# Attention in plain float32: unsplit operands for scores and values, the values' heads on halves of the columns

## The chip, the core and the metric

The kernel runs on one core of one Trainium2 chip. The core has a matrix engine, TensorE (PE in the profile, PEld for its weight loads), a vector engine (DVE), a scalar engine that also applies functions (ACT), GpSimd (POOL) and SyncE (SP), which here issues the transfers. The metric is the device time of one execution in microseconds (us). Before the change it is 951.21 us, the median of three runs from 950.32 to 952.36.

## What is computed

Two decoder layers over 256 tokens of width 1024, one sequence. Each layer is a half-step SwiGLU FFN, a token mixer, and another half-step FFN; the mixer of the first layer is stick-breaking attention, that of the second a gated linear recurrence. The part that is changed is the attention, with 16 heads of 64:

```python
q = qkv[0] * (SB_HEAD_DIM ** -0.5)
k, v = qkv[1], qkv[2]
for blk in range(S // Q_BLOCK):
    z = einsum('bhqd,bhkd->bhqk', q[:, :, t0:L], k[:, :, :L])
    log_keep = where(mask, log_sigmoid(-z), 0.0)
    later = cumsum(log_keep, axis=3, reverse=True) - log_keep
    w = where(mask, exp(log_sigmoid(z) + later), 0.0)
    outs.append(einsum('bhqk,bhkd->bhqd', w, v[:, :, :L]))
...
return o @ w_o
```

`Q_BLOCK` is 128, so there are two blocks. The product of queries and keys is called scores here, the product of the weights `w` and the values `v` is called values.

## The kernel before

Everything is float32. A projection multiplies a weight by an activation, and each is kept as a rounded part and a rest (`wh`, `wl` and the like, both in the type fp32r that PE streams in one pass). A product is then three matmuls, high by high, high by low and low by high, all into the same PSUM bank. The rounded part is written by ACT, the rest by DVE. Helpers do this: `load` for weights (L582 on ACT, L585 on DVE), `split` for activations, `Acc.group` for the three matmuls (L611). A product can also be given to PE in plain float32, with no split; the gates of the second layer do so (L1301).

Tokens lie along the columns: a tile is 128 channels by 256 tokens (T). Heads go in pairs, since two heads of 64 channels fill 128 partitions; tile `f` holds pair `f` (0 to 7), and `c` counts pairs of pairs (0 to 3), four heads. Keys and values come in two blocks of 128. The first block of keys serves all 256 queries, the second only the last 128, so each product comes in a wide form (256 columns) and a short one (128).

In `attention`:

- `q_proj(f)` projects queries and keys of pair `f`, and writes them as a high and a low tile (ACT, then DVE at L1069 or L1082).
- `v_proj(fp)` projects the values of four heads (L1042), and `v_out` writes them high and low (DVE at L1055).
- `scores(c)` first puts a mask into four PSUM banks (L1114), then adds the products of queries and keys (L1130): for each pair and block three matmuls for each of the two heads. A head has 64 channels, so the one head's operands sit on partitions 0 to 63 and the other's on 64 to 127; the two alternate and write to different banks. Then comes `softplus` (ACT and DVE).
- `sums(c, e)` adds the running sums into the same banks as a product with a triangle of ones (L1160, L1163), takes the exponential on ACT, and splits the resulting weights (ACT, and DVE at L1176).
- `values(f)` multiplies the values of both heads of pair `f`, 128 columns of stationary operand, by the weights of both heads side by side (L1190): three matmuls for each of the two blocks, 512 and 256 columns. Only the half in which head and weights belong together is used. ACT and DVE (L1198) copy that half out, high and low, once for each head.
- `down` is the output projection. It begins when some of the heads are done; `tail` puts the last values in behind its second weight tile.

What sets the order: the code records operations with a cost in nanoseconds each, and `Program.schedule` then places them engine by engine, by due times that follow from PE's recorded order and by when inputs and buffers come free. The costs are the third thing in each `pr.op` call. `hook(f)` records loads of modulation weights (`rawm`), each of which SP issues in its place and DVE reads (L645). SP's queue carries all weights (`raw`, three buffers, and `rawm`, four) in one order.

Of the kernel before, what the change touches and what calls it, by code (L numbers as in the profile page):

```python
# [14 lines left out]
P = 128  # L15
T = 256
# [27 lines left out]
SKIP = 1  # L44

# [361 lines left out]
def trunk(ctx, tc, first_in, cb, par, modw, gu, wdn, qk, wv, wo, win, wri, wout, out):  # L407
# [12 lines left out]
    def f32(ap):  # L420
        return ap.bitcast(F32)
# [589 lines left out]
    def attention(l, s, nxt, hook):  # L1011
        R, F = new_phase(94, 24)
# [36 lines left out]
        def v_out(fp):  # L1049
            acc, _ = vs[fp]  # L1050
            b = acc.b
            y = Buf(R, 4, name=f"vh{fp}"), Buf(R, 4, name=f"vl{fp}")
            rd = [(b, 0), (b, 1)]
            A(y[0], b, AF.Copy, 512, rd, [y[0]], psum=True)
            V(lambda: dve.tensor_tensor(y[1](), b(), f32(y[0]()), ALU.subtract), 512, rd + [y[0]], [y[1]])  # L1055
            vs[fp] = y
# [4 lines left out]
        def q_proj(f):  # L1061
            if f == 0:
                firsts.append(up_first((l, s), [q_load(i) for i in range(NFIRST)], (0.125, 1.0)))
            y = qs[f] = Buf(R, 4, name=f"qh{f}"), Buf(R, 4, name=f"ql{f}")
            if f < NFIRST:
                def put(g, t, rd, c):
                    cols = slice(g * T, (g + 1) * T)
                    A(lambda: y[0]()[:, cols], t, AF.Identity, T, [t, rd], [(y[0], g)], ptr=1, bias=c)
                    V(lambda: dve.scalar_tensor_tensor(y[1]()[:, cols], t(), c(), f32(y[0]()[:, cols]), ALU.add,  # L1069
                                                       ALU.subtract), T, [t, rd, (y[0], g)], [(y[1], g)])  # L1070

                for g, v in enumerate(next(firsts[0])):
                    put(g, *v)
                return
            acc = Acc(f"qk{f}")
            up(acc, q_load(f), (l, s), True)

            def put2(g, scale):
                b, rd = acc.b, (acc.b, (g, 0))
                cols = slice(g * T, (g + 1) * T)  # L1080
                A(lambda: y[0]()[:, cols], lambda: b()[:, cols], AF.Copy, T, [rd], [(y[0], g)], psum=True, scale=scale)
                V(lambda: dve.scalar_tensor_tensor(y[1]()[:, cols], b()[:, cols], scale, f32(y[0]()[:, cols]), ALU.mult,  # L1082
                                                   ALU.subtract), T, [rd, (y[0], g)], [(y[1], g)])

            for g in range(2):
                put2(g, (0.125, 1.0)[g])
# [14 lines left out]
        def scores(c):  # L1101
# [20 lines left out]
            def products():  # L1122

                for j, (qh, ql) in enumerate(pairs):
                    for i, (kc, qc) in enumerate(((slice(T, T + P), slice(0, T)), (slice(T + P, 2 * T), slice(P, T)))):
                        m = NC[i] // 2
                        for n, (v, w) in enumerate(((qh, qh), (qh, ql), (ql, qh))):
                            for e in range(2):
                                rows = slice(e * 64, (e + 1) * 64)
                                pe.matmul(zb[e][i]()[:, j * m : (j + 1) * m], v()[rows, kc], w()[rows, qc], start=False,  # L1130
                                          stop=j == 1 and n == 2, skip_group_check=True)

            pr.op("PE", 460.0 + 510.0 * len(fs), products, [q for r in pairs for q in r], [z for zz in zb for z in zz])
# [17 lines left out]
        def sums(c, e):  # L1151
            sp_ = ws_.pop((c, e))
            w = Buf(F, 6, name=f"w{c}{e}")
# [17 lines left out]
            if e == 0:  # L1171
                os_[c, "w"] = Buf(R, 12, name=f"wh{c}"), Buf(R, 12, name=f"wl{c}")
            y = os_[c, "w"]
            cols = slice(e * W2, (e + 1) * W2)
            A(lambda: y[0]()[:, cols], w, AF.Copy, W2, [w], [(y[0], e)])
            V(lambda: dve.tensor_tensor(y[1]()[:, cols], w(), f32(y[0]()[:, cols]), ALU.subtract), W2, [w, (y[0], e)], [(y[1], e)])  # L1176
# [406 lines left out]
```

## Time and profile before

| | |
|---|---|
| median of three runs | 951.21 us |
| the profiled execution's own time | 950.51 us |
| its span, first to last instruction | 948.7 us |
| PE busy | 938.9 us (99%) |
| DVE busy | 794.2 us (84%) |
| ACT busy | 568.2 us (60%) |
| granted PE clock, mean | 0.997 |
| attention (about 197 to 312 us), L1130, L1190, L1160 on the chain | 1%, 1%, 1% of the span rounded |

The chain of waits is followed back from the last instruction: at each step to what released it, or to the instruction ahead of it on its engine. A row of the chain gives the start and the length of a piece in us, then the engine, the tile, the line and how many instructions it holds. Rows of the timeline give the same with tiles and shapes; a matmul's own length there includes its way through the array, so the distance between starts tells what one costs. In rows by line, three numbers with strokes are the shortest, median and longest duration in ns. The waits of SP's queue name what held a transfer back: total us, times, longest.

### The profile page before, as it was taken

Reading aid. Unit: us, or ns where it says so; the run is one execution under the profiler, and the core shown is the slowest. Engines: PE = TensorE matmul, PEld = TensorE weight load, DVE = VectorE, ACT = ScalarE, POOL = GpSimd, SP = SyncE. Lnnn points to the kernel's source line nnn. Section 1 sums busy time; section 2 is a strip of 40 time slices with the busy share of each in tenths; the row PEclk is TensorE's granted clock in tenths of the full one; section 3 lists DMA queues with packets and bytes.
Section 4 is the critical chain, followed back from the end, with each engine's and each line's share of the span. In section 5 each row is a group of like instructions: output and inputs, shape, how many; then the busy total and the mean of one; then the engine's idle time right before and its main releaser. Section 6 shows DMA issues by size and latency. Waiting matters only on the chain.

```text
span 948.7 us, 19727 instructions
## 1 busy us (share of the span) xinstructions
PE 938.9 (99%) x8110; PEld 929.4 (98%) x8110; DVE 794.2 (84%) x1304; ACT 568.2 (60%) x934; POOL 2.4 (0%) x15
## 2 busy tenths in 40 slices
PE   8999999999999999999999999999999999999997
PEld 7999999999999999999999999999999999999996
DVE  8999987899999999888889998865999997555443
ACT  6784544488887755454367555535789676544343
POOL 1000000000000000000000000000000000000000
PEclk9999999999999999999999999999999999999998
DMA  9989989857744699989967998886253646545431
GB/s 366 404 327 371 349 330 358 326 206 278 266 145 168 227 341 346 344 320 347 351 236 285 354 361 326 333 335 233 89 181 131 223 175 242 206 180 204 170 113 45
DMA packets 48332, 251.25 MB, mean 265 GB/s; under 512 B 5361, under 2 KB 5745, under 8 KB 28530
## 3 DMA queue, kind: packets, MB, share of 16 engines
q1 hardware_dynamic: 47952, 249.59, 70.2%
q8 instruction: 63, 1.03, 0.4%
q10 hardware_dynamic: 290, 0.40, 0.1%
q14 instruction: 27, 0.22, 0.1%
HBM read 248.92 MB, written 1.05 MB: 263 GB/s over the span
## 4 chain that ended last, share of the span: by engine, by line
PE 97%; DVE 2%; DMA 1%; issue 0%; ACT 0%; SPq 0%; DVEq 0%
PE bank L611 90%; PE bank L1042 2%; PE bank L1301 1%; PE bank L1190 1%; PE bank L917 1%; PE bank L1130 1%; DVE wl L585 1%; PE bank L1160 1%; DMA arenar<-in_first_in 1%; DVE arenar L645 0%; DVE x L1413 0%; PE bank L1163 0%; PE bank L1114 0%; DVE arenaf L1385 0%; PE bank L704 0%
## 5 line engine op out<-in xcount | busy, mean ns | idle before, releaser
L611 PE MATMUL bank<-hx,wh 128*128 128x256 f32 (+1 forms) x3264 | 560.5, 277 | 0.2 <-DVE hx L941 0.2
L582 ACT ACTIVATE wh<-raw 128x1024 fp32r<-128x1024 f32 (+1 forms) x330 | 335.4, 1037 | 282.0 <-PE bank L611 191.9
L611 PEld LDWEIGHTS bank<-hx,wh 128*128 128x128 f32 x3264 | 493.7, 188 | 0.5 <-DVE hx L941 0.4
L585 DVE TENSOR_TENSOR wl<-raw,wh 128x1024 fp32r<-128x1024 f32 (+1 forms) x330 | 387.4, 1197 | 103.0 <-ACT wh L582 99.4
L611 PE MATMUL bank<-hx,wl 128*128 128x256 f32 (+1 forms) x1640 | 452.7, 277 | 0.0
L611 PEld LDWEIGHTS bank<-hx,wl 128*128 128x128 f32 x1640 | 308.3, 188 | 0.0
L611 PE MATMUL bank<-arenar,wh 128*128 128x256 f32 x1696 | 289.4, 276 | 0.0
L611 PEld LDWEIGHTS bank<-arenar,wh 128*128 128x128 f32 x1696 | 255.6, 188 | 0.0
L611 PE MATMUL bank<-arenar,wl 128*128 128x256 f32 x848 | 234.3, 276 | 0.1
L645 DVE SCALAR_TENSOR_TENSOR rawm<-rawm,cact 128x1024 f32<-128x1024 f32 x128 | 155.4, 1221 | 20.2 <-DMA rawm<-in_modw 20.1
L611 PEld LDWEIGHTS bank<-arenar,wl 128*128 128x128 f32 x848 | 159.3, 188 | 0.3 <-DVE wl L585 0.3
L554 ACT ACTIVATE arenar<-a 128x256 fp32r<-128x256 f32 x88 | 35.3, 405 | 11.8 <-DVE a L870 10.3
L875 DVE TENSOR_TENSOR arenar<-a,arenar 128x256 fp32r<-128x256 f32 x88 | 36.4, 421 | 0.5 <-ACT arenar L554 0.5
L554 ACT ACTIVATE sg<-bank 128x256 f32<-128x256 f32 x82 | 29.8, 367 | 9.6 <-PE bank L611 9.5
L870 DVE TENSOR_TENSOR a<-bank,sg 128x256 f32<-128x256 f32 x82 | 34.2, 420 | 0.4 <-ACT sg L554 0.2
L785 DVE SCALAR_TENSOR_TENSOR x<-bank,mf,x 128x256 f32<-128x256 f32 (+1 forms) x49 | 21.8, 475 | 9.2 <-PE bank L611 9.1
L554 ACT ACTIVATE hx<-x,mf 128x256 fp32r<-128x256 f32 x40 | 19.3, 499 | 16.3 <-DVE x L785 16.3
L554 ACT ACTIVATE hx<-hpre,mf 128x256 fp32r<-128x256 f32 x41 | 19.9, 502 | 11.0 <-DVE hpre L731 9.6
L1042 PE MATMUL bank<-wh,hx 128*128 128x256 f32 x128 | 23.4, 281 | 0.0
L645 DVE SCALAR_TENSOR_TENSOR arenar<-arenar,cact 128x1024 f32<-128x1024 f32 x16 | 19.5, 1222 | 1.6 <-DMA arenar<-in_first_in 1.6
L554 ACT ACTIVATE arenaf<-bank 128x512 f32<-128x512 f32 (+1 forms) x37 | 17.0, 512 | 6.0 <-DVE arenaf L1372 1.8
L1523 ACT ACT_TABLE_LOAD x15 | 19.2, 1283 | 1.6 <-PEq L1571 1.4
(130 smaller groups left out, 550.4 us busy)
## 6 DMA issues: line engine op xcount, KB each, us to landing
raw<-in_gu SPq DMA_DIRECT2D x79, 1024.0 KB, 5.2
rawm<-in_modw SPq DMA_DIRECT2D x128, 512.0 KB, 7.0
raw<-in_wdn SPq DMA_DIRECT2D x44, 1024.0 KB, 5.2
raw<-in_win SPq DMA_DIRECT2D x10, 1024.0 KB, 4.9
arenar<-in_first_in SPq DMA_DIRECT2D x16, 512.0 KB, 8.3
raw<-in_qk SPq DMA_DIRECT2D x8, 1024.0 KB, 4.8
raw<-in_wout SPq DMA_DIRECT2D x5, 1024.0 KB, 4.9
raw<-in_first_in SPq DMA_DIRECT2D x8, 512.0 KB, 8.9
```

The costliest lines, as they stand in the source:

```text
L554: act.activation(o(), i(), f, **{k: (v() if callable(v) else v) for k, v in kw.items()})
L582: act.activation(h()[:, :m], raw()[:, a : a + m], AF.Copy)
L585: dve.tensor_tensor(lo()[:, :m], raw()[:, a : a + m], f32(h()[:, :m]), ALU.subtract)
L611: pe.matmul(o(b()), wc(u()), xc(v()), start=start and n == 0, stop=stop and n == len(passes) - 1, skip_group_check=True)
L645: dve.scalar_tensor_tensor(raw(), raw(), 1.0, cact(), ALU.mult, ALU.mult, accum_out=m()[:, t : t + 1])
L785: dve.scalar_tensor_tensor(x[d]()[:, w], acc.b()[:, j * T + w.start : j * T + w.stop], gate()[:, d : d + 1], x[d]()[:, w], ALU.mult, ALU.add)
L870: V(lambda: dve.tensor_tensor(a(), b()[:, T:], sg(), ALU.mult), T, [(b, (1, 0)), sg], [a])
L875: V(lambda: dve.tensor_tensor(y[1](), a(), f32(y[0]()), ALU.subtract), n, [a, y[0]], [y[1]])
L917: pr.op("PE", c_mm(T, 4), lambda: pe.matmul(b()[:, g * T : (g + 1) * T], raw()[:, c0 : c0 + P], h0(), start=start, stop=False, skip_group_ ...
L1042: pe.matmul(o, u()[:, tb * P : (tb + 1) * P], v()[:, c0 : c0 + 256], start=start and n == 0, stop=k == KD - 1 and n == 2, skip_group_check ...
L1130: pe.matmul(zb[e][i]()[:, j * m : (j + 1) * m], v()[rows, kc], w()[rows, qc], start=False, stop=j == 1 and n == 2, skip_group_check=True)
L1523: act.preload_act_table_set(TABLES[t])
```

## The change

Scores are computed by one plain float32 matmul for each head, pair and block in place of three split ones; queries and keys are no longer split, so ACT alone writes them. The values and the attention weights are not split either. `values` is called once for four heads and writes one PSUM bank: for each pair and block, each head's 64 values are the stationary operand, on columns 0 to 63 or 64 to 127 of the array, multiplied by that head's weights only; the two heads alternate. The outputs are evicted and split in one piece of 128x512. The two buffers of the phase change size, the costs given to the planner are two constants, and the calls stand in another order.

```diff
+SCORES = 1400.0
+VALUES = 1350.0
...
-        R, F = new_phase(94, 24)
+        R, F = new_phase(50, 68)
...
         def v_out(fp):
-            y = Buf(R, 4, name=f"vh{fp}"), Buf(R, 4, name=f"vl{fp}")
-            rd = [(b, 0), (b, 1)]
-            A(y[0], b, AF.Copy, 512, rd, [y[0]], psum=True)
-            V(lambda: dve.tensor_tensor(y[1](), b(), f32(y[0]()), ALU.subtract), 512, rd + [y[0]], [y[1]])
-            vs[fp] = y
+            y = vs[fp] = Buf(F, 4, name=f"v{fp}")
+            A(y, b, AF.Copy, 512, [(b, 0), (b, 1)], [y], psum=True)
...
             def products():
 
-                for j, (qh, ql) in enumerate(pairs):
+                for j, y in enumerate(pairs):
                     for i, (kc, qc) in enumerate(((slice(T, T + P), slice(0, T)), (slice(T + P, 2 * T), slice(P, T)))):
                         m = NC[i] // 2
-                        for n, (v, w) in enumerate(((qh, qh), (qh, ql), (ql, qh))):
-                            for e in range(2):
-                                rows = slice(e * 64, (e + 1) * 64)
-                                pe.matmul(zb[e][i]()[:, j * m : (j + 1) * m], v()[rows, kc], w()[rows, qc], start=False,
-                                          stop=j == 1 and n == 2, skip_group_check=True)
-
-            pr.op("PE", 460.0 + 510.0 * len(fs), products, [q for r in pairs for q in r], [z for zz in zb for z in zz])
+                        for e in range(2):
+                            rows = slice(e * 64, (e + 1) * 64)
+                            pe.matmul(zb[e][i]()[:, j * m : (j + 1) * m], y()[rows, kc], y()[rows, qc], start=False, stop=j == 1,
+                                      skip_group_check=True)
+
+            pr.op("PE", SCORES, products, pairs, [z for zz in zb for z in zz])
...
-            A(lambda: y[0]()[:, cols], w, AF.Copy, W2, [w], [(y[0], e)])
-            V(lambda: dve.tensor_tensor(y[1]()[:, cols], w(), f32(y[0]()[:, cols]), ALU.subtract), W2, [w, (y[0], e)], [(y[1], e)])
-
-        def values(f):
-            wh, wl = os_[f // 2, "w"]
-            vh, vl = vs[f // 2]
+
+        def values(c):
+
+            ww = [ws_.pop((c, e, "w")) for e in range(2)]
+            v = vs[c]
             b = Buf(banks)
 
             def fn():
-                for tb in range(2):
-                    vc = slice(tb * T + (f % 2) * P, tb * T + (f % 2 + 1) * P)
-                    o = b() if tb == 0 else second(b())
-                    m = NC[tb] // 2
-                    at = BL[tb].start + (f % 2) * m
-                    for i, (u, v) in enumerate(((vh, wh), (vh, wl), (vl, wh))):
-                        pe.matmul(o, u()[:, vc], v().rearrange("p (e s) -> p e s", e=2)[:, :, at : at + m],
-                                  start=tb == 0 and i == 0, stop=i == 2, skip_group_check=True)
-            pr.op("PE", c_mm(512) + c_mm(T), fn, [vh, vl] + [(q, e) for q in (wh, wl) for e in range(2)], [b])
...
+                for j in range(2):
+                    for tb in range(2):
+                        at = BL[tb].start + j * NC[tb] // 2
+                        for e in range(2):
+                            vc = tb * T + j * P + e * 64
+                            pe.matmul(b()[e * 64 : (e + 1) * 64, j * T + tb * P : (j + 1) * T], v()[:, vc : vc + 64],
+                                      ww[e]()[:, at : at + NC[tb] // 2], start=j == tb == 0, stop=j == tb == 1,
+                                      skip_group_check=True)
+            pr.op("PE", VALUES, fn, [v] + [(w, i) for w in ww for i in range(2)], [b])
+            y = Buf(R, 4, name=f"oh{c}"), Buf(R, 4, name=f"ol{c}")
+            A(y[0], b, AF.Copy, 512, [b], [y[0]], psum=True)
+            V(lambda: dve.tensor_tensor(y[1](), b(), f32(y[0]()), ALU.subtract), 512, [b, y[0]], [y[1]])
+            for j in range(2):
+                os_[2 * c + j] = y, slice(j * T, (j + 1) * T)
...
         sums(2, 1)
         q(7)
         scores(3)
+        values(2)
         v_proj(3)
```

What this does to the order of the instructions is seen at three places. The first is on PE, where the scores of the last two pairs are computed, `scores(3)`. Before, part of the last value projection (L1042, `wh` and `wl` with `hx`) stands between the masks (L1114) and the products (L1130); banks 70, 68, 67 and 69 take the scores.

```order
L1114 MATMUL bank_69<-mask,ident 128x256
L1042 MATMUL bank_64<-wh_81,hx 128x256
...
L1042 MATMUL bank_64<-wh_81,hx 128x256
L1130 MATMUL bank_70<-arenar_2524 128x256
L1130 MATMUL bank_68<-arenar_2524 128x256
L1130 MATMUL bank_70<-arenar_2524 128x256
L1130 MATMUL bank_68<-arenar_2524 128x256
L1130 MATMUL bank_70<-arenar_2524 128x256
L1130 MATMUL bank_68<-arenar_2524 128x256
L1130 MATMUL bank_67<-arenar_2524 128x128
```

After, at the same place, with L1104 the masks, L1173 the values of pairs 4 and 5 and L1119 the scores of pairs 6 and 7:

```order
L1104 MATMUL bank_65<-mask,ident 128x256
L1173 MATMUL bank_70<-arenaf_2525 64x256 x2
L1173 MATMUL bank_70<-arenaf_2525 64x128 x2
L1173 MATMUL bank_70<-arenaf_2525 64x256 x2
L1173 MATMUL bank_70<-arenaf_2525 64x128 x2
L1119 MATMUL bank_63<-arenaf_2525 128x256
L1119 MATMUL bank_69<-arenaf_2525 128x256
L1119 MATMUL bank_67<-arenaf_2525 128x128
L1119 MATMUL bank_65<-arenaf_2525 128x128
L1119 MATMUL bank_63<-arenaf_2525 128x256
L1119 MATMUL bank_69<-arenaf_2525 128x256
L1044 MATMUL bank_66<-wh_81,hx 128x256
```

The values moved to directly ahead of the scores' products, and the value projection (L1044, L1042 before) begins behind them.

The second place is on PE in the output projection, around the last values. Before, with L1190 the values of pair 7 and L611 the projection's steps (`wh_80` to `wh_83` with their `wl` are the last four of its eight weight halves; the first step that needs pair 7 has `wh_83`):

```order
L1190 MATMUL bank_66<-arenar_2524 128x512 x3
L1190 MATMUL bank_66<-arenar_2524 128x2x128 x3
L611 MATMUL bank_65<-arenar_2524,wh_80 128x256 x2
...
L611 MATMUL bank_65<-arenar_2524,wh_82 128x256 x2
...
L611 MATMUL bank_65<-arenar_2524,wh_83 128x256 x2
```

After, with L1173 the values of pairs 6 and 7 and L613 the steps (the first that needs pair 6 has `wh_82`):

```order
L1173 MATMUL bank_69<-arenaf_2525 64x256 x2
L1173 MATMUL bank_69<-arenaf_2525 64x128 x2
L613 MATMUL bank_67<-arenar_2524,wh_78 128x256 x2
...
L613 MATMUL bank_67<-arenar_2524,wh_79 128x256 x2
...
L613 MATMUL bank_64<-arenar_2524,wh_80 128x256 x2
...
L613 MATMUL bank_64<-arenar_2524,wh_81 128x256 x2
...
L613 MATMUL bank_64<-arenar_2524,wh_80 128x256 x2
...
L613 MATMUL bank_64<-arenar_2524,wh_82 128x256 x2
```

Between the last values and the first step that needs them stand seven steps of three matmuls before, and five after.

The third place is on SP's queue, at the loads of the last value projection (`wv`) and of the output projection (`wo`). Before (L547) and after (L549):

```order
L547 DMA raw_73<-in_wv 128x2048
L547 DMA rawm_76<-in_modw 128x1024
L547 DMA rawm_77<-in_modw 128x1024
L547 DMA raw_71<-in_wo 128x2048
L547 DMA raw_72<-in_wo 128x2048
```

```order
L549 DMA raw_73<-in_wv 128x2048
L549 DMA rawm_74<-in_modw 128x1024
L549 DMA rawm_75<-in_modw 128x1024
L549 DMA rawm_76<-in_modw 128x1024
L549 DMA raw_71<-in_wo 128x2048
L549 DMA rawm_77<-in_modw 128x1024
L549 DMA raw_72<-in_wo 128x2048
```

Two more modulation tiles (`rawm`) stand ahead of the second `wo` load than before. Further up and down the queue single `rawm` loads have changed places with `raw` loads in the same way; no load is added or removed.

More of the change, by code (lines that the diff above doesn't have):

```diff
@@ L1228, in attention @@
         q(6)
-        values(2)
+        values(1)
         sums(2, 0)
-        values(3)
         sums(2, 1)
```

45 lines of the change are left out of this document (11 added, 34 removed).

## The prediction

> **What bounds the kernel now.** I read the page first, for the engine that carries the span, then the stretch in which attention runs, then the chain of waits inside it. Engines, the clock row and the chain by engine:
>
> ```profile
> PE 938.9 (99%) x8110; PEld 929.4 (98%) x8110; DVE 794.2 (84%) x1304; ACT 568.2 (60%) x934; POOL 2.4 (0%) x15
> ...
> PE 97%; DVE 2%; DMA 1%; issue 0%; ACT 0%; SPq 0%; DVEq 0%
> ```
>
> TensorE (PE) carries 97% of the chain. Attention lies between 197 and 312 us; busy time in that stretch:
>
> ```profile
> core 0: us, PE busy (x) PEld busy (x) DVE busy (x) ACT busy (x) POOL busy (x), PEclk, DMA share, GB/s
> 197.40:312.40 115.00, 115.00 (x993) 111.80 (x992) 109.29 (x192) 96.04 (x173) 0.00 (x0) 1.00 0.57 204
> ```
>
> PE is busy for all 115.00 us at full clock. DVE, at 109.29 of them, comes near, but PE never waits for it. So here time is gained or lost only by what PE's own instructions take, unless a new wait appears. The chain shows the groups that the change touches (start, length, line, count), and, from the second layer, plain float32 products (L1301):
>
> ```profile
> 210.08 5.49 PE bank L611 x48
> 215.57 0.45 PE bank L1114 x4
> 216.03 1.52 PE bank L1130 x24
> 217.55 5.69 PE bank L611 x48
> ...
> 249.45 1.05 PE bank L1190 x6
> ...
> 690.61 1.73 PE bank L1301 x8
> 692.34 5.49 PE bank L611 x48
> ```
>
> A projection's matmul of 256 columns (L611) takes 5.49/48 = 0.114 us. The 24 matmuls of the scores (L1130), half of them 256 wide and half 128, would take 12 x 0.114 + 12 x 0.057 = 2.06 us one after the other; they took 1.52, and the 48 behind them 0.20 longer than usual. Rows of the timeline in short windows around that group show both things (start, length):
>
> ```profile
> 215.65 0.38 PE L1114 MATMUL bank<-mask,ident 128*128 128x256 bf16 x2
> ...
> 215.75 0.27 PE L1114 MATMUL bank<-mask,ident 128*128 128x256 bf16 x1
> 215.96 0.38 PE L1130 MATMUL bank<-arenar 64*128 64x256 f32 x2
> ...
> 216.18 0.40 PE L1130 MATMUL bank<-arenar 64*128 64x256 f32 x4
> ...
> 216.41 0.33 PE L1130 MATMUL bank<-arenar 64*128 64x128 f32 x4
> ...
> 216.47 0.39 PE L1130 MATMUL bank<-arenar 64*128 64x128 f32 x4
> ...
> 216.58 0.44 PE L1130 MATMUL bank<-arenar 64*128 64x128 f32 x4
> ...
> 217.27 0.27 PE L1130 MATMUL bank<-arenar 64*128 64x128 f32 x2
> ...
> 217.48 0.38 PE L611 MATMUL bank<-hk,wh 128*128 128x256 f32 x1
> ...
> 217.70 0.28 PE L611 MATMUL bank<-hk,wh 128*128 128x256 f32 x1
> ```
>
> First, "x2" at 215.96: the two heads of a pair, on the upper and the lower 64 rows, run abreast. Second, going in and out of halves costs. In: last mask to first pair 0.21 instead of the 0.10 between masks, first to second pair 0.22 instead of 0.114. Out: 0.21 from the last pair, after 0.11 between short pairs, then 0.22 instead of 0.114. That is about 0.20 at either boundary. From the last mask (215.75) to the second L611 (217.70) are 1.95 us; less one mask (0.11) and one L611 (0.12) a scores group costs **1.72**, of it 0.39 boundaries and 1.33 stream.
>
> **The change part by part.** Scores: for each group of four heads 24 split matmuls become 8 plain ones. A plain product of 256 columns is two records; L1301's eight records take 1.73, so 0.216 each and 0.43 a product. No row has a plain product of 128 columns. It costs between half (0.22) and as much as the wide one (0.43). I take half, since the short pairs above stand 0.06 to 0.11 apart where wide ones stand 0.114: width does shorten the stream. If both heads run abreast as in L1130, a group streams 2 x (0.43 + 0.22) = 1.30, with boundaries 1.69: 0.03 less than 1.72, times 4 is **-0.1**. The ends: 0.29 more each if the two heads run staggered (below, +1.2); with the short product at 0.43, 0.43 more each (+1.7).
>
> Values: before, a call (L1190) is 1.05 for two heads, so 2.10 us for a group of four, on the full array without a boundary; it computes each head's values against both heads' weights and throws half away. After, eight plain products for a group, each on 64 of the columns. Abreast they stream 1.30, like the scores. Row halves run abreast in the rows above, column halves are in no row, so the ends are 1.30 abreast and 2 x 2 x (0.43 + 0.22) = 2.60 in turn. I take abreast: the nearest row is L1130, the array halved the other way. The boundary too is in no row: between 0 and the 0.39 of L1130; I take 0.39. So 1.69 against 2.10, times 4 is **-1.6** (ends: -3.2 without boundaries, +3.6 in turn with them). As the order shows, the values of the third group stand right ahead of the scores of the fourth, which joins two boundaries into one: **-0.2** (end 0).
>
> The Trainium skill (TensorEngine Tiling (Array Packing), Key Properties) says that changing the tiling mode drains the engine. The rows in and out of L1130 agree, at 0.2 us a boundary. By that rule the column halves pay as the row halves do and the sum is the one here; were it to hold for rows alone, the sum would be 1.6 lower.
>
> Splits that go: the weights' (L1176), the values' (L1055), the keys' and queries' (L1082, L1069); outputs' (L1198) become four of 128x512; rows by line:
>
> ```profile
> L1176 DVE TENSOR_TENSOR arenar<-arenaf,arenar x8: 947/958/959, 233.3 to 287.9; 128x768 fp32r<-128x768 f32 x8
> ...
> L1055 DVE TENSOR_TENSOR arenar<-bank,arenar x4: 685/689/693, 217.2 to 284.1; 128x512 fp32r<-128x512 f32 x4
> ...
> L1198 DVE TENSOR_TENSOR arenar<-bank,arenar x16: 408/420/429, 253.1 to 297.1; 64x256 fp32r<-64x256 f32 x16
> ...
> L1082 DVE SCALAR_TENSOR_TENSOR arenar<-bank,arenar x12: 405/422/425, 218.9 to 272.0; 128x256 fp32r<-128x256 f32 x12
> ```
>
> On DVE that frees 8 x 0.958 + 4 x 0.689 + 12 x 0.422 + 16 x 0.420 = 22.2 us (and four queries' splits more), less 4 x 0.689 = 2.8 for the new ones. ACT loses eight copies of 128x768 and twelve small evictions. All of it counts **0**: PE waited for neither engine in these 115 us, and it does not come back as time. It buys slack instead: transfers in this stretch mostly wait for DVE to release a weight buffer, so they can start earlier.
>
> ```profile
> SPq L547 <- DVE wl L585: 95.8, 19, 11.3
> SPq L547 <- DVE rawm L645: 19.1, 12, 3.4
> ```
>
> Moved transfers: on SP's queue some modulation tiles now go ahead of the last query/key, output-projection and next-FFN weights; each must find its buffer read by DVE (L645, longest wait 3.4). Cost 0 while the three weight buffers run ahead; bounded by one such wait on PE, +3.4, and not below 0, since PE waits for no transfer here.
>
> Down projection: the last values group must reach the seventh head pair's step. Before, the last one left PE at 295.75 and its last split ended at 297.06 + 0.43:
>
> ```profile
> 294.69 1.05 PE bank L1190 x6
> 295.75 1.26 PE bank L611 x11
> ...
> 297.06 0.43 DVE L1198 TENSOR_TENSOR arenar<-bank,arenar 64x256 fp32r<-64x256 f32 x1 [0.38 <-ACT arenar L554]
> ```
>
> That is 1.74 us of latency for four small evictions. Now one eviction and one split (0.69) of 512 stand there, and PE has five steps of three matmuls (15 x 0.114 = 1.71) plus the 0.2 of the boundary as cover. Cost 0, at worst one weight split (about 1.2) in the way.
>
> **Sum**: -0.1 - 1.6 - 0.2 = -1.9 us. The profiled execution took 950.51 (span 948.7); the median of the runs is 951.21, 0.70 above it, so I forecast 951.21 - 1.9 = **949.3**, which is 0.2% less, on the edge of what a measurement of this kernel tells from no change (about 1.9 us; its three runs spread over 2.0).
>
> **The rivals.**
> *Staggered halves.* A plain product is two records, and the first head's two stand ahead of the second head's. If matmuls start strictly in order, the second head cannot start before the first head's second record, and with widths that alternate they never close up: counting in records of 0.108, starts fall so that eight products end after 15 instead of 12, i.e. 1.62. Then scores cost 2.01 (+0.29), values 2.01 (-0.09): 4 x 0.20 - 0.2 = +0.6, so 951.8, no change. For it: two records for one product are in L1301's count. Against it: nothing, but L1130's pairs are single records and cannot show it. The Trainium skill (TensorE: Matmul & The Clock Gate, Part 3) says that matmuls keep program order in start and end; by that rule this is the outcome, and no row here decides whether it holds across halves.
> *No boundary for column halves.* L1190's neighbours in the new order are projections, as L1130's were, so I would expect one; without it 951.21 - 0.1 - 3.2 = 947.9, faster.
> *Columns in turn*, on the other side. If the second head's products cannot stream while the first's do, values cost 2.60 + 0.39 = 2.99 per group against 2.10, +3.6 in all, and -0.3 for the rest makes 954.5; with staggered scores 955.7. It turns to slower once a values group takes more than about 2.6. For it: two streams then enter over the same 128 rows, where L1130's used 64 each. Against: the outputs are separate.
> *A new wait* at the down projection or the moved transfers: +1.2 to +3.4, so 950.5 to 952.7. Against: DVE has some 20 us less to do there.
>
> **How the numbers follow.** Forecast (abreast, boundaries paid) 0.34, taken half on each side of the edge but for a little more on the faster one; no boundary 0.20; staggered 0.23; columns in turn 0.18; a new wait 0.05. Faster: 0.20 + 0.22 = 0.42. Same: 0.12 + 0.22 = 0.34. Slower: 0.18 + 0.06 of staggered and waiting = 0.24. The range reaches from the case without boundaries, less the spread of the runs (947.2), to the middle of columns in turn (955.0); the likeliest case by itself is 948.3 to 950.3.
>
> **What would show it.** Values' groups on the chain at about 1.3 (of 1.7 with boundaries) mean abreast; 1.6 staggered; 2.6 in turn. Scores' groups against 1.52 tell staggered from abreast by themselves. L611 groups behind the values at 5.69 instead of 5.49 show the boundary. In the stretch PE should still have no wait, and DVE should fall to about 90 us. I am wrong if PE waits there at all, or if the stretch shrinks by more than 4 us.

## The result, and the profile after

The changed kernel takes **949.48 us**, the median of 20 runs (948.41 to 950.76), against 951.08 us (950.32 to 953.83) for 20 runs of the kernel before: a ratio of 0.9983, with a 95% interval from 0.9977 to 0.9989. That is 1.6 us less, with an interval from 1.0 to 2.2; forecast were 1.9. The profiled execution took 950.72 us, 1.24 above its own median.

The page of the kernel after, engines and chain by engine:

```profile
PE 938.7 (99%) x8094; PEld 927.0 (98%) x8094; DVE 777.7 (82%) x1264; ACT 558.9 (59%) x914; POOL 2.4 (0%) x15
...
PE 97%; DMA 1%; DVE 1%; ACT 0%; SPq 0%; DVEq 0%; issue 0%
```

PE still carries 97% of the chain, and its busy time as a whole reads the same (938.7 against 938.9). A difference of 2 us has to be looked for in the stage. The two profiled executions start differently: on the chains, the sum of squares ahead of attention (two matmuls, L696 before, L698 after) comes 2.0 us later in this execution of the kernel after. Near the start, before and after, the first 32 matmuls (L917, L919) stand so:

```profile
10.68 7.17 PE bank L917 x32
```

```profile
11.46 8.86 PE bank L919 x32
```

They begin 0.78 later, since the load ahead of them lands later, and take 1.69 longer: from 10.6 to 18 us the mean granted clock was 1.00 in the execution before and 0.77 in the one after. Some 0.5 us of this is made up on the way to attention. It goes with the execution and not with the change: among the kernels below that have the changed attention, the 32 take 7.17 in some profiles and 8.86 in others. The start of attention, before:

```profile
197.13 0.24 PE bank L696 x2
...
312.43 0.24 PE bank L696 x2
```

And after, with the groups of attention between the two sums (L613 is the projections' line, L611 before; L1119 the scores; L1173 the values):

```profile
199.13 0.24 PE bank L698 x2
...
218.02 1.51 PE bank L1119 x16
219.53 5.69 PE bank L613 x48
...
240.34 1.45 PE bank L1173 x16
241.79 5.68 PE bank L613 x48
...
271.73 0.46 PE bank L1104 x4
272.19 1.45 PE bank L1173 x16
273.64 1.51 PE bank L1119 x16
...
284.59 8.83 PE bank L613 x75
293.43 1.45 PE bank L1173 x16
294.88 17.58 PE bank L613 x150
...
312.45 0.24 PE bank L698 x2
```

From one sum of squares to the other, called the stretch from here on, are 312.43 - 197.13 = 115.30 us before and 312.45 - 199.13 = 113.32 us after: **1.98 us less**. (The rows are rounded; unrounded the latter is 113.33, and stretches and differences from here on are from unrounded times, so they can differ by 0.01 from the rows.) The group of scores takes 1.51 (1.52 before), the group of values 1.45 (2 x 1.05 before). What follows attention takes the same within 0.3 us in all; the rest of the difference between the spans (948.7 and 949.0) lies in the 2.0 us ahead of attention.

The stretch in windows of the kernel after (columns as shown of before):

```profile
198.96:312.29 113.33, 113.33 (x979) 108.31 (x978) 94.54 (x158) 84.96 (x153) 0.00 (x0) 1.00 0.57 212
```

PE is busy all the time at full clock, DVE has fallen from 109.29 (in 115.00) to 94.54, not to the 90 that was forecast, since 16 modulation tiles instead of 13 (1.22 us each) are now read in the stretch, and ACT from 96.04 to 84.96. All waits of PE in the whole kernel after:

```profile
PE bank L919 <- DVE hpre L738: 2.1, 1, 2.1
PE bank L1412 <- POOL eps L509: 1.2, 1, 1.2
```

Both lie in the first 12 us of the kernel; in attention PE waits for nothing. Rows of the timeline of the kernel after, in short windows in and around one group of values, answer whether the halves of the columns run abreast (start, length):

```profile
240.06 0.28 PE L613 MATMUL bank<-hx,wl 128*128 128x256 f32 x1
240.27 0.44 PE L1173 MATMUL bank<-arenaf 128*64 128x256 f32 x2
...
240.54 0.39 PE L1173 MATMUL bank<-arenaf 128*64 128x256 f32 x2
...
241.40 0.39 PE L1173 MATMUL bank<-arenaf 128*64 128x128 f32 x4
...
241.51 0.28 PE L1173 MATMUL bank<-arenaf 128*64 128x128 f32 x2
241.72 0.39 PE L613 MATMUL bank<-hk,wh 128*128 128x256 f32 x1
...
241.94 0.28 PE L613 MATMUL bank<-hk,wh 128*128 128x256 f32 x1
```

"x2" at 240.27 and at 240.54 are the same record of both heads, begun together. The second record of the first product begins 0.27 later, the short ones 0.11 apart. The first records of a pair are 0.007 apart by the unrounded starts. The boundary is there too: 0.21 from the last projection to the first pair, 0.21 from the last pair to the next projection, 0.22 to the one behind it, where 0.114 is the usual distance.

### The profile page after: what moved, and what is told of

Same layout as the page of the kernel before. It is cut to its first block, busy times and chain, and to the rows that moved or that the text cites. A ratio compares the mean times of both kernels' runs of the same rounds, so it can differ in the third digit from the quotient of the medians.

```text
span 949.0 us, 19623 instructions
## 1 busy us (share of the span) xinstructions
PE 938.7 (99%) x8094; PEld 927.0 (98%) x8094; DVE 777.7 (82%) x1264; ACT 558.9 (59%) x914; POOL 2.4 (0%) x15
## 3 DMA queue, kind: packets, MB, share of 16 engines
HBM read 248.92 MB, written 1.05 MB: 263 GB/s over the span
## 4 chain that ended last, share of the span: by engine, by line
PE 97%; DMA 1%; DVE 1%; ACT 0%; SPq 0%; DVEq 0%; issue 0%
PE bank L613 90%; PE bank L1044 2%; PE bank L919 1%; PE bank L1279 1%; DMA raw<-in_gu 1%; DMA arenar<-in_first_in 1%; PE bank L1119 1%; PE bank L1173 1%; PE bank L1149 1%; DVE wl L587 0%; DVE arenar L647 0%; DVE x L1391 0%; PE bank L1152 0%; PE bank L1104 0%; PE bank L706 0%; PE bank L698 0%
## 5 line engine op out<-in xcount | busy, mean ns | idle before, releaser
L613 PE MATMUL bank<-hx,wh 128*128 128x256 f32 (+1 forms) x3264 | 560.4, 277 | 0.0
L613 PEld LDWEIGHTS bank<-hx,wh 128*128 128x128 f32 x3264 | 493.3, 188 | 0.0
L613 PE MATMUL bank<-hx,wl 128*128 128x256 f32 (+1 forms) x1640 | 452.7, 277 | 0.0
L613 PEld LDWEIGHTS bank<-hx,wl 128*128 128x128 f32 x1640 | 308.4, 188 | 0.0
L613 PE MATMUL bank<-arenar,wh 128*128 128x256 f32 x1696 | 289.8, 276 | 0.0
L613 PEld LDWEIGHTS bank<-arenar,wh 128*128 128x128 f32 x1696 | 255.7, 188 | 0.2 <-issue 0.2
L613 PE MATMUL bank<-arenar,wl 128*128 128x256 f32 x848 | 234.5, 276 | 0.1
L613 PEld LDWEIGHTS bank<-arenar,wl 128*128 128x128 f32 x848 | 159.3, 188 | 0.3 <-DVE wl L587 0.3
L556 ACT ACTIVATE arenaf<-bank 128x256 f32<-128x256 f32 (+1 forms) x53 | 23.3, 487 | 12.5 <-PE bank L613 5.1
L1044 PE MATMUL bank<-wh,hx 128*128 128x256 f32 x128 | 23.0, 279 | 0.0
```

What stands on the lines that cost most here:

```text
L556: act.activation(o(), i(), f, **{k: (v() if callable(v) else v) for k, v in kw.items()})
L613: pe.matmul(o(b()), wc(u()), xc(v()), start=start and n == 0, stop=stop and n == len(passes) - 1, skip_group_check=True)
L1044: pe.matmul(o, u()[:, tb * P : (tb + 1) * P], v()[:, c0 : c0 + 256], start=start and n == 0, stop=k == KD - 1 and n == 2, skip_group_check ...
```

## Experiments

Each kernel is the kernel after with one edit, unless said otherwise. "Stretch" is read as above, in the profiled execution of each kernel; times and ratios are against runs of the kernel before on the same chip.

### The two products apart

The scores' part undone: three split matmuls for each product again, with the queries' and keys' splits.

```diff
-            y = qs[f] = Buf(F, 4, name=f"q{f}")
+            y = qs[f] = Buf(R, 4, name=f"qh{f}"), Buf(R, 4, name=f"ql{f}")
...
-                        for e in range(2):
-                            rows = slice(e * 64, (e + 1) * 64)
-                            pe.matmul(zb[e][i]()[:, j * m : (j + 1) * m], y()[rows, kc], y()[rows, qc], ...
+                        for n, (v, w) in enumerate(((qh, qh), (qh, ql), (ql, qh))):
+                            for e in range(2):
+                                rows = slice(e * 64, (e + 1) * 64)
+                                pe.matmul(zb[e][i]()[:, j * m : (j + 1) * m], v()[rows, kc], w()[rows, qc], ...
```

> The change without its scores part: queries and keys split again and three matmuls per product (L1130's form), values as in the changed kernel. Theory (only PE's own groups count): a scores group takes 1.52 us on the chain either way (1.51 in the changed kernel), so the attention stretch between the two sums of squares stays at 113.3 to 113.6 us (changed kernel 113.3, before 115.3) and the time is 1.3 to 1.9 us under before. Rival (the freed DVE and ACT work is part of the gain): the 7 us of DVE splits that return give back a third of the gain, so about 1 us under before and a stretch near 114.

It took 949.22 us against 950.92 (0.9982, 0.9974 to 0.9991), with a stretch of 113.47. On its chain:

```profile
218.00 1.52 PE bank L1130 x24
```

The stretch is 0.14 longer, but most of this is not the scores' own. At `scores(3)` three matmuls of the value projection now stand between values and scores, so that the two groups no longer share a boundary; from the masks there to the end of that value projection it is 9.32 us against 9.22 in the kernel after. The first three groups together give the scores' part, about 0.04 us: plain float32 is worth next to nothing here, and nothing that the time shows.

The values' part undone: split values and weights, both heads' columns at once on the full array, two calls in the place of each new one.

```diff
-            ww = [ws_.pop((c, e, "w")) for e in range(2)]
-            v = vs[c]
+            wh, wl = os_[f // 2, "w"]
+            vh, vl = vs[f // 2]
...
+                    for i, (u, v) in enumerate(((vh, wh), (vh, wl), (vl, wh))):
+                        pe.matmul(o, u()[:, vc], v().rearrange("p (e s) -> p e s", e=2)[:, :, at : at + m],
...
-        values(0)
+        (values(0), values(1))
```

> The change without its values part: weights and values split again, values on the full array (L1190's form), scores in plain float32 as in the changed kernel. Theory: the values' groups go back from 1.45 plus boundaries to 2.10 us, so the stretch is 115.0 to 115.3 us and the time within 0.4 us of before. Rival (freed work): the splits of queries and keys are still gone, so about a third of the gain, 0.5 us or more, stays.

It took 950.54 us against 950.92 (0.9997, 0.9988 to 1.0006), with a stretch of 115.22. On its chain:

```profile
240.44 2.10 PE bank L1182 x12
242.54 5.49 PE bank L613 x48
```

Nearly all of the gain is the values': 115.22 - 113.33 = 1.89 us. A group falls by 0.65, and the projections behind it take 5.68 instead of 5.49, so about 0.46 are left of each. Four times 0.46 and the joined boundary of 0.2 would be 2.0.

### Plain float32 or the halves

Which half of the values' edit gains? Plain float32 with the old shape, that is the full array, both heads' weights side by side and half of the products thrown away; scores as in the kernel after.

```diff
-                            pe.matmul(b()[e * 64 : (e + 1) * 64, j * T + tb * P : (j + 1) * T], v()[:, vc : vc + 64],
-                                      ww[e]()[:, at : at + NC[tb] // 2], ...
+                    pe.matmul(o, v()[:, vc], w().rearrange("p (e s) -> p e s", e=2)[:, :, at : at + m], ...
```

> The changed kernel with the values in plain float32 but on the full array, both heads' values against both heads' weights as before, 512 and 256 columns; scores as in the changed kernel, outputs evicted a head at a time. Theory (the gain is that of the column halves, plain float32 by itself costs a third more): a group of two heads takes 4/3 of 1.05, about 1.3 to 1.4 us, four heads 2.6 to 2.8 without boundaries against 1.45 and boundaries of 0.39; the stretch is 116.3 to 117.5 and the time 1.0 to 2.2 us over before. Rival (plain float32 is what gains, having no split operands): stretch at or under 115.3, time not over before.

It took 953.35 us against 951.13 (1.0024, 1.0013 to 1.0035), with a stretch of 117.57. On its chain:

```profile
239.12 2.58 PE bank L1174 x8
```

Plain float32 alone loses: 2.58 against the 2.10 of the split form, 1.23 times as much where a third more was expected. Two heads abreast halve the plain products' stream (2.58 / 2 = 1.29), and that is the gain. Of the stretch's 2.35 over the run with split values, 4 x 0.48 = 1.92 are the groups; the rest is the output projection's last 144 matmuls, 17.11 against 16.69, a matter taken up below. No run has the split form on halves of the columns, so what that would take stays open.

### In turn instead of alternating

All products of the first head, then all of the second; first in the values, then in the scores.

```diff
-                for j in range(2):
-                    for tb in range(2):
-                        at = BL[tb].start + j * NC[tb] // 2
-                        for e in range(2):
+                for e in range(2):
+                    for j in range(2):
+                        for tb in range(2):
+                            at = BL[tb].start + j * NC[tb] // 2
```

> The changed kernel with the values' matmuls of one head all ahead of those of the other, instead of by turns; same work. Theory (the halves run abreast because neighbours in the order lie on different halves): a values group goes from 1.45 to about 2.7 us, 4 times 1.3 = +5 us against the changed kernel, about 3.4 us (0.36%) over before. Rival (the array takes matmuls out of order across halves): still 1.45 a group, time 1.6 us under before.

It took 952.10 us against 950.92 (1.0012, 1.0003 to 1.0021), with a stretch of 116.57. The group on its chain:

```profile
238.53 2.15 PE bank L1173 x16
```

That is 0.7 more than alternating, but not the 1.3 of two streams end to end. (Four times 0.7 are 2.8 of the stretch's 3.24; the other 0.44 are the last 150 projection matmuls, 18.02 instead of 17.58, taken up below.) Its timeline in short windows shows why:

```profile
238.25 0.28 PE L613 MATMUL bank<-hx,wl 128*128 128x256 f32 x1
238.46 0.43 PE L1173 MATMUL bank<-arenaf 128*64 128x256 f32 x1
...
239.16 0.44 PE L1173 MATMUL bank<-arenaf 128*64 128x256 f32 x2
```

Until 239.16 one record at a time begins; then two begin together. By count and widths the pair holds the fifth of the first head's eight records and the first of the second head's: to three digits they begin at 239.162 and 239.168, and the first head's sixth, ahead of the latter in the program, only at 239.378. So a matmul for the other half overtakes three that wait for the busy half. The first head's four records alone take 0.70, then the second head's eight 1.30, and with the way in 2.15.

The scores, with the same edit in `products`:

```diff
-                for j, y in enumerate(pairs):
-                    for i, (kc, qc) in enumerate(...):
-                        m = NC[i] // 2
-                        for e in range(2):
-                            rows = slice(e * 64, (e + 1) * 64)
+                for e in range(2):
+                    rows = slice(e * 64, (e + 1) * 64)
+                    for j, y in enumerate(pairs):
+                        for i, (kc, qc) in enumerate(...):
+                            m = NC[i] // 2
```

> The changed kernel with the scores' matmuls of one head all ahead of those of the other, on the row halves; same work. Theory: a scores group goes from 1.51 to about 2.8 us, +5 us against the changed kernel, about 3.4 us over before. Rival: still 1.51, time 1.6 us under before.

It took 952.38 us against 950.92 (1.0013, 1.0004 to 1.0022), with a stretch of 116.33. On its chain:

```profile
233.33 2.26 PE bank L1119 x16
```

Rows and columns behave alike: 0.75 more for a group, where 1.3 was expected. In its first group too the second head's first record begins beside the first head's fifth (218.138 and 218.132).

If up to three waiting records are overtaken, then two products of a head (four records) ahead of the other head's should cost next to nothing.

```diff
-                    for tb in range(2):
-                        at = BL[tb].start + j * NC[tb] // 2
-                        for e in range(2):
+                    for e in range(2):
+                        for tb in range(2):
+                            at = BL[tb].start + j * NC[tb] // 2
```

> The changed kernel with the values' heads alternating after two products (four records) instead of one. In the run with the heads in turn the second head's first matmul began beside the fifth of the first head's eight records. Theory (matmuls of the other half may pass up to about four that wait for a busy half): a values group stays at 1.45 to 1.5 us on the chain, stretch 113.3 to 113.5. Rival (only one waiting matmul may be passed): the second head begins two records late, a group takes about 1.75 us, stretch 114.5.

One execution took 950.17 us, with a stretch of 113.93. On its chain and in its timeline:

```profile
239.20 1.50 PE bank L1173 x16
...
293.94 17.97 PE bank L613 x150
```

```profile
238.92 0.28 PE L613 MATMUL bank<-hx,wl 128*128 128x256 f32 x1
239.13 0.44 PE L1173 MATMUL bank<-arenaf 128*64 128x256 f32 x2
```

The group takes 1.50, as the look-ahead has it, and its first records begin together although three others stand between them. The stretch is longer than expected by some 0.4, and this is the last row: 150 projection matmuls take 17.97 instead of 17.58. That is taken up below.

### The freed time of DVE and ACT

Splits of the size of the removed ones are computed again, into buffers that nobody reads: all of them on DVE, and on ACT the weights' copies.

```diff
+        def spare_split(y, n, cells, parts=1):
...
+                    A(h, y, AF.Copy, n, [y], [h])
+                    V(lambda h=h, lo=lo: dve.tensor_tensor(lo(), y(), f32(h()), ALU.subtract), n, [y, h], [lo])
...
+            spare_split(y, 512, 4)
...
+            spare_split(w, W2, 6)
```

> The changed kernel with the removed splits of weights, values, queries and keys computed again on ACT (8 copies of 128x768) and DVE (28 subtractions, some 17 us), their results unused; PE's matmuls are the changed kernel's. Theory (only PE's own groups count): DVE in the stretch rises by some 17 us, PE still waits for nothing, the stretch stays at 113.3 to 113.4 us and the time 1.3 to 1.9 us under before. Rival (the freed work is part of the gain): a wait on PE appears and the stretch grows by 0.5 us or more.

It took 949.11 us against 951.31 (0.9980, 0.9971 to 0.9989). DVE and ACT in a window that begins and ends some 2.5 us ahead of its stretch:

```profile
197.00:310.00 113.00, 113.00 (x977) 108.02 (x976) 108.40 (x187) 90.48 (x161) 0.00 (x0) 1.00 0.58 207
```

Between the marks themselves it is 108.36 for DVE and 91.01 for ACT (109.59 and 96.34 before), and the stretch stays at 113.33. So DVE's work is back nearly in full and ACT's about half, and neither costs anything: the work taken off them is worth nothing here.

### Places and boundaries

The values at their old places, each behind the next sums or projections.

```diff
-        values(0)
         q(5)
         v_proj(2)
+        values(0)
         sums(1, 0)
```

> The changed kernel with the values' calls at the places that they had before. Theory: the matmuls are the same, but no values group stands next to a scores group, so one boundary of 0.2 us more, stretch 113.5, time 1.4 us under before. Rival (the new order carries a large part of the gain): PE waits in the stretch and most of the gain is lost.

It took 949.45 us against 951.31 (0.9982, 0.9973 to 0.9991), with a stretch of 113.51. That is the number expected, but partly by luck: its last 150 projection matmuls take 18.02 on the chain where the kernel after has 17.58, and the 84 ahead of the last values 9.54, 0.114 each, where the kernel after's 75 take 8.83, 0.118 each. The two all but cancel (+0.44 and -0.35), and about the boundary of 0.2 is left.

More groups joined: the scores of a later group are moved right ahead of the values, so that two boundaries become one.

```diff
-        scores(1)
         q(4)
+        scores(1)
         values(0)
...
-        scores(2)
         q(6)
+        scores(2)
         values(1)
+        q(7)
         sums(2, 0)
         sums(2, 1)
-        q(7)
+        v_proj(3)
         scores(3)
         values(2)
-        v_proj(3)
```

> The changed kernel with the calls in another order, so that three of the four values groups stand next to a scores group instead of one. Theory (each boundary into or out of halves costs about 0.2 us, two neighbours share one): two more boundaries go, the stretch falls from 113.3 to 112.9 us, the time is 2.0 us under before. Rival: going from column halves to row halves drains as well, in full, so nothing is gained; or scores and values now wait for exponentials and the stretch grows by the wait.

Against the plan only two of the three groups stood next to each other (the scores and values at 237.00, below, and those at 259.06); the third pair was parted by half a projection. It took 949.36 us against 951.31 (0.9985, 0.9970 to 1.0000), with a stretch of 112.84.

```profile
237.00 1.51 PE bank L1119 x16
238.50 1.45 PE bank L1173 x16
239.96 5.68 PE bank L613 x48
...
291.31 1.45 PE bank L1173 x16
292.76 17.57 PE bank L613 x150
```

Where they are joined nothing stands between the groups and only one 5.68 behind both: about 0.2 saved. What is saved is one way out. The step from row halves to column halves is not free: from the last pair of scores (238.225) to the first pair of values (238.433) are 0.21 us, as from a projection, where short pairs are 0.10 apart. One boundary less than in the kernel after gave 0.49 in the stretch, though; 0.2 were to be had from it. About another 0.2 are in 51 projection matmuls that took 5.99 us behind the third values, 0.114 each less the 0.2 of the boundary, where those ahead of the last values take 0.118 in the kernel after. With all three joined, by the same moves for the first two and this for the third:

```diff
         values(1)
+        v_proj(3)
         sums(2, 0)
         sums(2, 1)
         q(7)
         scores(3)
         values(2)
-        v_proj(3)
```

> The order meant for the joined run, where by an oversight only two of the four values groups stood next to a scores group: here it is three, against one in the changed kernel. Theory (a boundary shared saves about 0.2 us): 0.2 us under the run with two joined, stretch 112.6, time about 2.2 us under before. Rival (what that run gained beyond the one boundary came from elsewhere in its order): stretch between 112.6 and 113.1; or a new wait for exponentials.

It took 949.37 us against 951.13 (0.9984, 0.9972 to 0.9997), with a stretch of 112.95 instead of 112.6: a miss. One more boundary had gone, and the stretch was longer. The row that makes it so is the last of these:

```profile
280.21 7.70 PE bank L613 x66
...
292.51 1.45 PE bank L1173 x16
293.96 18.02 PE bank L613 x150
```

18.02 against 17.57 in the run with two joined and 17.58 in the kernel after, for the same matmuls. Less the 0.2 of the boundary, that is 0.119 us for one against 0.116 on average. By the starts in the traces the difference lies in the first hundred or so: they are 0.118 apart here and 0.113 in the other two; the last fifty are about 0.12 apart in all three.

What sets this pace? The last run adds to the three joined groups one matmul of 64 columns, with zeros as operand, six matmuls behind the last values. The kernel has such matmuls at other places already (`kick_op`; 0.04 to 0.05 us each). The text below gives the 150 as 17.92 and 17.48, 0.1 less than the chain has for them.

```diff
             if post is not None:
                 post(c)
+                if c == 1:
+                    b, j = place[0]
+                    pr.op("PE", 0.0, lambda b=b, j=j: pe.matmul(b.b()[:, j * T : j * T + 64], zero[:, :P], ident[:, :64], ...
```

> The kernel with three values groups next to scores, and one matmul of 64 columns more, with zeros as operand, put behind the last values group, ahead of the down projection's last 150 matmuls. Open is why these 150 took 17.92 us there and 17.48 in the kernel after the change, with the same instructions. Theory: TensorE keeps one of two paces from one disturbance to the next, and a short matmul is such a disturbance; then the 150 take about 17.5, the stretch of attention falls from 12.95 above a hundred to 112.6 us, and the time is about 2.2 us under the kernel before. Rival: the pace belongs to the buffers and transfers of that stretch; then they stay at 17.9, the stretch at 113.0 (0.05 for the added matmul), and the time at 1.7 under the kernel before.

It took 948.12 us against 950.71 (0.9970, 0.9955 to 0.9986), with a stretch of 112.66. On its chain (L822 is the added matmul):

```profile
291.95 1.45 PE bank L1177 x16
293.40 0.90 PE bank L613 x6
294.31 0.04 PE bank L822
294.35 16.77 PE bank L613 x144
```

The 150 now take 0.90 + 16.77 = 17.67 with the boundary, 0.35 less than 18.02, for 0.04 of added matmul. In one and the same trace, the last starts ahead of the added matmul are 0.118 apart, and a few matmuls behind it they are 0.113 apart. Every other instruction is there as often as in the run with three joined, and the transfers go out in the same order, so the pace does not belong to them; in this one profiled execution a short matmul switched it. It is the fastest kernel of this study, by its median and by its stretch; its interval overlaps those of the kernel after and of the run with three joined, with which it was not timed side by side.

| kernel | scores group, us | values group, us | stretch, us | ratio to before |
|---|---|---|---|---|
| before | 1.52 | 2.10 | 115.30 | 1 |
| after | 1.51 | 1.45 | 113.3 | 0.9983 |
| scores split again | 1.52 | 1.45 | 113.47 | 0.9982 |
| values split, full array | 1.51 | 2.10 | 115.22 | 0.9997 |
| values plain, full array | 1.51 | 2.58 | 117.57 | 1.0024 |
| values in turn | 1.51 | 2.15 | 116.57 | 1.0012 |
| scores in turn | 2.26 | 1.45 | 116.33 | 1.0013 |
| three joined, one matmul added | 1.51 | 1.45 | 112.66 | 0.9970 |

## Why the prediction was right

*The bound.* That only PE's own instructions count in this stage held: PE has no wait there, and with DVE's work put back the stretch stayed the same. The splits' 0 was right.

*Scores, -0.1.* Measured: a group of 1.51 instead of 1.52, 4 x 0.01; of the 0.14 us of stretch when it is undone, the greater part is the joined boundary that went with it. The plain product of 128 columns, which no row of before showed, costs half the wide one: the last short pairs begin 0.11 apart, a record each.

*Values, -1.6, and joined boundaries, -0.2.* Undoing both costs 1.89 us of stretch, so the two terms together were right. A group is 1.45 on the chain, the way in included, and the projections behind it take 0.2 more: 1.65, against the 1.69 that was worked out. That the boundaries of the row halves would hold for column halves too was a choice between 0 and 0.39, and they did: 1.65 - 1.30, about 0.35. The Trainium skill (TensorEngine Tiling (Array Packing), Key Properties) has a change of the tiling mode drain the engine; both ways of halving agree here, at some 0.2 us a boundary. Between values and scores one boundary is left of two. The joined boundary shows directly in the rows at 272.19 and 273.64, where scores begin as the values end.

*Staggered halves, chance 0.23.* It fell. The heads' records begin together in scores and values, though a product is two records. The prediction had nothing against this rival but the single records of L1130, so that its main case came true on this point was a choice and not a finding. The runs in turn show that the rival's condition does not hold: matmuls do not start strictly in the order of the program when they use different halves. The Trainium skill (TensorE: Matmul & The Clock Gate, Part 3) says that they keep that order in start and end; here the measurement decides against it, with a matmul begun at 239.168 that stands behind one begun at 239.378.

*Columns in turn, 0.18, and no boundary, 0.20.* Both fell by the first rows of a values group. Forcing the heads in turn shows that the price of that rival was also too high: 2.15 a group and not 2.60 + 0.39, since half of the first head's stream is overlapped all the same.

*A new wait, 0.05.* None. SP's waits for the readers of weights and of modulation tiles in the stretch of the kernel after:

```profile
SPq L549 <- DVE wl L587: 88.2, 15, 13.8
...
SPq L549 <- DVE rawm L647: 5.4, 6, 2.0
```

The modulation tiles wait 5.4 us in all where it was 19.1, and PE waits for none of the transfers. (The 95.8 of the prediction for weights covers a window up to 330 us; in the stretch it is 86.9 before, so the waits for weights did not become shorter.) At the down projection the new eviction and split are done in time, by its timelines of ACT and of DVE:

```profile
294.92 0.60 ACT L556 ACTIVATE arenar<-bank 128x512 fp32r<-128x512 f32 x1 [4.87 <-PE bank L1173]
```

```profile
295.55 0.69 DVE L1179 TENSOR_TENSOR arenar<-bank,arenar 128x512 fp32r<-128x512 f32 x1 [2.91 <-ACT arenar L556]
```

From the last values (294.88) to the end of the split (296.24) are 1.36 us, within the 1.91 of cover that was counted.

*The total.* The stretch fell by 1.98 against 1.9 forecast, and the time by 1.6, with an interval from 1.0 to 2.2 that holds both. The chances were split at a fall of about 1.9, 0.42 faster and 0.34 no change: 1.6 lies on the less likely side of that edge, though with 20 runs the interval leaves out no change. That 949.48 lies 0.2 from the 949.3 forecast is partly luck. What the sum did not hold is the projections' pace: it moves single runs of the stage by 0.3 to 0.5 us, a quarter of the whole gain, more than the 0.08 by which the stage's forecast missed. The granted clock near the start moves the profiled executions by 1.7 us.

## What to carry to other kernels

Two small products that need only half of the array's columns (or rows) run abreast here if they alternate, and on column halves still when two plain products (four records) of the one stand ahead of the other. This, not the plain float32, made the values' gain. Each visit to the halves cost about 0.35 us, of which two neighbouring groups save 0.2, so groups of that kind belong next to each other. Work taken off an engine that nobody waited for was worth nothing, and putting it back unused is a cheap way to know. For an edit of 2 us in 950, compare one stage between two fixed marks, and look at the pace of the unchanged matmuls beside it before a few tenths are put down to the edit.

## What was not expected of the hardware

In these runs TensorE looks ahead across halves, of the rows as of the columns: with eight records of one head ahead, the other head's first began beside the fifth and so overtook three; with four ahead, it began together with the first.

The same 256-column matmuls run at more than one steady pace at the full clock. The 150 behind the last values took 17.57 or 17.58 us in the kernel after and in four of the runs, and 17.97 or 18.02 in four others (values in turn, values by fours, old places, three joined); by their starts, the first hundred or so stand 0.113 apart in the former and 0.118 in the latter. One matmul of 0.04 us took the last of these back to 0.113 within a few matmuls. It is not the place alone: ahead of the last values, 75 took 8.83 in the kernel after (0.118 each), and 66 took 7.70 with three groups joined (0.114 each, less the 0.2 of the boundary). Nor does it need halves: with plain values on the full array, too, the last 144 took the slower pace (17.11 against 16.69 with split ones). What in the sequence sets the pace at a given place was not found.
